# One block of value products for each quad of attention, behind all of its transposes

## Chip, cores and metric

The kernel runs on one core of a Trainium2 chip. The metric is device time in microseconds of one launch, the median of three runs.

## What is computed

One inference step of a small hybrid transformer: 128 context tokens and 512 latent tokens, model width 1024, two layers, each with three groups of attention heads side by side and a squared-ReLU MLP of width 4096. All in float32. The part that matters here is the attention:

```
# differential heads (4): two softmaxes, one subtracted from the other
p1 = softmax(q1 @ k1.T * scale);  p2 = softmax(q2 @ k2.T * scale)
o  = (p1 - lam * p2) @ v
# windowed heads (8, two key/value heads): context keys + three blocks of 128 keys + a sink logit
p  = softmax(concat([s_ctx, s_band, s_sink]));  o = p[ctx] @ cv + p[band] @ vb
# latent heads (4): keys and values unpacked from a compressed vector
o  = softmax(q @ k.T * scale) @ v
```

A latent token reads 128 context keys and 512 latent keys (five blocks of 128), in the windowed heads three or four blocks. Each head's values have 64 columns.

## The kernel before

Everything up to the MLP of a layer is a plan: tasks are given in a serial order with their engine, an assumed duration, a priority and the tiles that they read, write and open. `Plan.run` (line 165) places them on the engines by readiness and priority, and emits each engine's instructions in the order in which the tasks start in that plan. An engine then runs its list strictly in order. A task's own instructions stay together. Rings (`RINGS`, line 46) limit how many tiles of a kind are open at once: `PT` 3, `t` (PSUM buffers for transposes and small products) 3, `o` (PSUM output) 1, `s` (scores) 2, `quad` (probabilities) 2, `E` 4.

The attention is cut into quads (`quad`, line 968): two heads times two blocks of 128 queries. In a layer there are eight quads of windowed, four of differential and four of latent heads. For each of the four (head, query block) pairs of a quad PE makes scores into `s` (lines 1000, 1008, 1016), DVE takes the maximum (1030), ScalarE the exponential with its sum (1038), and the row is scaled (965) or, in differential heads, the second softmax is subtracted (1060). The probabilities lie in `e_`, a tile of the ring `quad`.

Then come the key blocks of the quad, in `slots` (line 1069): five for differential and latent heads, four for windowed ones (three that both query blocks read, and one that only one reads). For each slot there are three tasks: `tr` on PE transposes two or four 128x128 blocks into a `t` buffer (line 1081), DVE or ScalarE evicts them into a `PT` buffer (the copy in line 1092; the profile has it under the helper's lines 376 and 374), and `pv` on PE adds the value products of the slot to O (line 1085): for each head one product, whose 64 output columns fill one half of O's partitions. Each such product is two records in the trace. `tr` and `pv` have the same priority, so the plan takes `pv` of a slot as soon as it is ready. O (ring `o`) is opened by the first `pv` and evicted after the last (line 1097 or the split in line 1100). The context's own queries have their own small path (`context`, line 1139).

Work of low priority fills PE's gaps: conditioning vectors (`conditioning`, lines 551 and 556) and parts of the output projection (`w_out`, lines 517 to 519). All DMA is issued from SyncE's queue (`dma`, line 379). The MLP behind the plan is written out in order and keeps PE busy throughout.

Of the kernel before, what the change touches and what calls it, by code (L numbers as in the profile page):

```python
# [17 lines left out]
PSUM = bass.MemoryType.PSUM  # L18

P = 128  # L20
DEPTH = 2
D = 1024
# [4 lines left out]
EPS = 1e-6  # L27
# [3 lines left out]
# columns of the input projection that go through one PSUM bank together  # L31
# [3 lines left out]
# key blocks of the windowed heads, [cache | L0..L3 | cache]: first column and block numbers per query block  # L35
# [9 lines left out]
# buffers of each ring  # L45
RINGS = {"E": 4, "X": 5, "PT": 3, "B": 8, "h": 4, "mix": 3, "quad": 2, "QK": 4, "wr": 3, "wh": 4, "wl": 4, "zin": 2, "sq4": 2,
         "stt": 10, "osb": 1, "Kc": 1, "ds": 2, "sm": 4, "rsq": 3, "Vsw": 1, "Vda": 1, "Vml": 1, "ckT": 1, "kz": 1,
         "s": 2, "t": 3, "o": 1, "z": 4}
# rings that share the tiles of one, and rings whose tiles are opened in the order of the plan or of priority
SHARE = {"h": "B", "mix": "B", "quad": "B", "QK": "B"}  # L50
IN_ORDER = {"h", "mix", "quad", "QK", "Vml", "Kc", "ds", "osb", "zin", "sq4", "wr", "wh", "wl"}
# microseconds: what one engine's result takes to reach another, the start of a transfer, bytes per microsecond
# [5 lines left out]
# How a layer is run: the engines of the hi and lo parts of operands and of the softmax's scaling, the priorities of  # L58
# transposes and of the preparation of operands, and the order of the parts: N conditionings (cN), half the query
# blocks of two windowed (s), differential (d) or latent (m) heads, their preparation (D, V, M), output projection (w)  # L60
# [35 lines left out]
class Slot:  # L96
    """A tile that one task opens and that is free again behind its last user."""
# [19 lines left out]
class Plan:  # L117
    """Orders the instructions of a phase: tasks are given in a serial order with what they read and write;
    run() places them on the engines by readiness and priority, and emits them in the order they start."""
# [7 lines left out]
    def held(self, ring, t):  # L127
        """A tile that is open already."""
        s = Slot(ring, None, t)
        self.slots.append(s)  # L130
        return s
# [33 lines left out]
    def run(self):  # L165
        """Tiles are opened ahead of the plan's order only where every task before them in that order can still
        have its own, so the order always ends."""
        free = dict(RINGS)
# [10 lines left out]
        rings = {}  # L179
# [22 lines left out]
        def blocked(t):  # L202
            """The ring that has no tile for a task yet."""
            need = {}
            for s in t.alloc:
                for q in s.rings:
                    need[q] = need.get(q, 0) + 1
            if "s" in need and z_left[0]:
                return "z"
            for q, c in need.items():  # L210
                if free[q] < c:
                    return q
            for q, c in need.items():
                before = [s for s in live[q] if not s.open and s.first < t.n]
                if before and (q in IN_ORDER or (q == "t" and t.prio >= 2e6 and free[q] == c)):
                    return q
                if not before:
                    continue
                ahead = [s for s in live[q] if s.open]
                for s in before:  # L220
                    n = sum([x.first <= s.first and x.last >= s.first for x in live[q]])
                    n += sum([x.first > s.first for x in ahead])
                    if n + c > RINGS[q]:
                        return q
            return None
# [9 lines left out]
        # the banks of "z" become those of "s"  # L235
# [14 lines left out]
        # the tensor engine's clock halves behind a window of little work, until a busy one  # L250
# [88 lines left out]
def tile_hybrid_step(ctx: ExitStack, tc: tile.TileContext, i, o):  # L339
# [25 lines left out]
    def add(*a, **k):  # L365
        return cur[0].add(*a, **k)
# [17 lines left out]
    def split(n, hi, lo, src, r, w, prio, scale=None, hi_alloc=(), lo_alloc=(), sb=None, extra=0.0):  # L384
        """hi = f32r(src * scale), lo = src * scale - hi: together the exact float32 value. All arguments are
        functions that give the operands. sb: the engines of hi and lo for a source in SBUF."""
        def f_hi(e):
            if e is S:
                S.activation(out=hi(), in_=src(), func=AF.Copy, scale=1.0 if scale is None else scale)  # L389
            else:  # L390
                e.tensor_copy(hi(), src())

        def f_lo(e):
            if scale is None:
                sub(e, lo(), src(), hi().bitcast(F32))
            else:
                e.scalar_tensor_tensor(out=lo(), in0=src(), scalar=scale, in1=hi().bitcast(F32),
                                       op0=ALU.mult, op1=ALU.subtract)

        wh, wl = w  # L400
        for eng, f, dur, rd, wr, al in (
                (sb[0] if sb else "A", f_hi, {"A": tA(n) + extra, "V": tV2(n)}, list(r), wh, hi_alloc),
                (sb[1] if sb else "V", f_lo, {"V": tV(n), "G": tG(n)}, list(r) + [wh], wl, lo_alloc)):
            if len(eng) > 1:
                add(eng, {e: dur[e] for e in eng}, f, r=rd, w=[wr], alloc=al, prio=prio)
            else:
                e = {"A": S, "V": V, "G": G}[eng]
                add(eng, dur[eng], lambda f=f, e=e: f(e), r=rd, w=[wr], alloc=al, prio=prio)
# [34 lines left out]
    # the sinks as three bfloat16 parts on the first three partitions, that ones sum up again  # L443
# [59 lines left out]
    def load_split(src, n, prio, k=1, load_prio=None, after=(), sb=None):  # L503
        """Weights as hi and lo slots; views with k feature tiles."""
# [10 lines left out]
    def mm3(out, w, a, first, last):  # L515
        """out += whi*ahi + whi*alo + wlo*ahi, w stationary."""
# [8 lines left out]
    def conditioning(l, sec, f0, prio, nf=2, wide=False):  # L525
        """nf feature tiles of one section."""
# [52 lines left out]
    def rsqrt(ms, n, r, prio, scale=1.0, eps=None):  # L579
        """Returns a function that gives y, and what its readers read."""  # L580
# [33 lines left out]
    def stat(st, k, hf, prio):  # L614
        """One feature tile's part of the sums of squares of a half of the tokens: all but the last tile are summed
        before the matrix product over the partitions."""
# [24 lines left out]
    def rstd(st, hf, rb, prio):  # L641
        """1/rms of the half's tokens, the same on all partitions, into PSUM."""
# [27 lines left out]
    def emit_h(l, n, hf, rb, h, k, prio):  # L670
        """h = x * rstd * A + B as hi + lo."""
# [86 lines left out]
    def projection(l, h):  # L758
        """Token-major input projection, with norms, rotary positions and the operands of the heads."""
# [14 lines left out]
        # caches  # L774
# [193 lines left out]
    def quad(l, kind, u, hd, vt, vcols, mix, kt_mix, pr_, hs, at):  # L968
        """Half pr_ of the query blocks of two heads; half 0 also takes the context's own queries."""
# [8 lines left out]
        for y in range(2):  # L978
            for x in range(2):
# [11 lines left out]
                for j in range(2 if kind == "da" else 1):  # L991
# [20 lines left out]
                    else:  # L1012
                        def scores(s=s, h=h, q=q, n=n, a=a, tiles=tiles, w=w, we=we):
# [4 lines left out]
                            # a bank of its own starts anew; the scores' own bank has this column unwritten  # L1018
# [55 lines left out]
        for z, (kt, have) in enumerate(slots):  # L1074
# [8 lines left out]
            def pv(z=z, kt=kt, c=c, w=w, PT=PT):  # L1083
                for x in range(2):
                    T.matmul(out=O.t[64 * x:64 * x + 64, c:c + w], lhsT=vt.t[:, kt, vcols[x]:vcols[x] + 64],  # L1085
                             rhs=PT.t[:, x, c:c + w], start=(z == 0), stop=(z == ns - 1))

# [5 lines left out]
            add("P", 0.23 * len(have), pv, r=[PT, (vt, kt)], w=[] if z == 0 else [O], alloc=[O] if z == 0 else [], prio=p_t)  # L1093
# [10 lines left out]
        if kind == "da":  # L1104
            # per-head rms norm; rows carry their softmax sum s1, so eps becomes eps * s1^2
# [108 lines left out]
    def da_prep(l, w, u, at):  # L1214
# [15 lines left out]
        for t in (1, 2, 3, 4, 0):  # L1230
            for a in range(2):
# [9 lines left out]
                def part(x, st=st, a=a):  # L1241
                    """The queries as [hi lo hi lo], the keys as [hi hi lo lo]."""
# [39 lines left out]
    def mla_prep(l, w, u, u0, kvw, at):  # L1282
# [8 lines left out]
        # rotary part of the keys: the same rows for every head  # L1291
# [135 lines left out]
    def up_out(gt, f, hf, puv, r):  # L1427
        """Squared ReLU of a feature tile, as hi + lo, in four stages."""
# [9 lines left out]
    def first_up(l, h, Gt, ws, after):  # L1438
        """The first half of the tokens goes feature tile by feature tile of h, into four accumulators."""
# [71 lines left out]
    # ================= layers =================  # L1511
    dn, Gt_last = None, None
    for l in range(DEPTH + 1):
        with ExitStack() as es:
# [52 lines left out]
            # attention  # L1567
# [49 lines left out]
            # norm and the first feature tiles  # L1617
# [20 lines left out]
        with ExitStack() as es:  # L1638
# [14 lines left out]
            # the banks of scores and outputs of the attention come first: the others are still read  # L1653
# [169 lines left out]
```

## Time and profile before

| | us |
|---|---|
| median of three runs | 1797.12 |
| lowest and highest run | 1793.64, 1797.24 |
| span of the profiled execution | 1794.8 |
| PE busy in it | 1701.9 |
| DVE busy in it | 1111.0 |
| ScalarE busy in it | 731.7 |

The span goes from the first to the last instruction of the profiled execution. In layer 0 the attention fills roughly 178 to 433 us, in layer 1 1055 to 1296 us; between and behind them lie the MLPs (475 to 890 us and 1345 to 1770 us, PE busy throughout). A busy PE is not PE at its peak: matmuls overlap in the pipeline and their ends are modelled, so the cost of one is read from the distance of starts, or from the pieces of the chain, which don't overlap. "PE" is the matmul, "PEld" its weight load; a table by stretch has PE, PEld, DVE, ScalarE (ACT) and GpSimd (POOL) in this order, then the granted TensorE clock (1.00 is the 2.4 GHz level, 0.50 the 1.2 GHz one), the DMA share and GB/s. The chain is the work that ended last, followed back from the end, at each step to what released it.

### The profile page before, as it was taken

How to read it: one execution, taken by the hardware profiler on the slowest of the kernel's cores; microseconds unless marked ns; L12 is line 12 of the kernel's file. 1: busy time of each engine (PE TensorE's matmuls, PEld its weight loads, DVE VectorE, ACT ScalarE, POOL GpSimd, SP SyncE). 2: the span in 40 equal slices, each digit the busy share in tenths (PEclk: the TensorE clock that was granted, in tenths of full speed). 3: DMA queues.
4: the chain of work that ended last, by engine and by line, in shares of the span. 5: the costliest groups of instructions: out<-in, count | busy, mean ns of one | idle time of the engine just before them, and what ended most of it. 6: DMA issues, size and time to landing. Idle time of an engine off the chain costs nothing.

```text
span 1794.8 us, 29510 instructions
## 1 busy us (share of the span) xinstructions
PE 1701.9 (95%) x11371; PEld 1509.7 (84%) x11371; DVE 1111.0 (62%) x2870; ACT 731.7 (41%) x1624; POOL 322.2 (18%) x284
## 2 busy tenths in 40 slices
PE   6999998999999999999989999989989999999997
PEld 4787567577999999999978766766879999999997
DVE  5875568887654444444594748988784444444446
ACT  4533566774432222322243336766653222321231
POOL 2310037422200000000063201653350000000000
PEclk9999999999999999999999999989999999999999
DMA  8323453431122222222212324303212222222221
GB/s 308 108 68 118 157 162 92 133 126 60 52 71 83 71 71 83 71 75 72 78 52 83 94 96 128 119 26 113 71 60 72 82 71 83 72 71 75 79 71 60
DMA packets 67388, 163.22 MB, mean 91 GB/s; under 512 B 6896, under 2 KB 31280, under 8 KB 67248
## 3 DMA queue, kind: packets, MB, share of 16 engines
q1 hardware_dynamic: 67248, 161.34, 27.7%
q8 instruction: 90, 1.47, 0.3%
q14 instruction: 50, 0.41, 0.1%
HBM read 153.15 MB, written 8.16 MB: 90 GB/s over the span
## 4 chain that ended last, share of the span: by engine, by line
PE 80%; DVE 14%; ACT 2%; issue 2%; POOL 1%; DMA 1%; SPq 0%; DVEq 0%; ACTq 0%; POOLq 0%
PE pu L518 15%; PE pu L519 15%; PE pu L517 15%; PE O L1085 4%; PE pt L1081 3%; PE pz L810 3%; PE pz L812 3%; PE pz L811 3%; PE po L517 2%; PE pa L551 2%; PE po L518 2%; PE po L519 2%; PE sps L1016 2%; PE sps L1008 1%; DVE stt L1030 1%
## 5 line engine op out<-in xcount | busy, mean ns | idle before, releaser
L517 PE MATMUL pu<-hh,wh 128*128 128x256 f32 (+1 forms) x960 | 299.2, 312 | 0.0
L519 PE MATMUL pu<-hh,wl 128*128 128x256 f32 (+1 forms) x960 | 299.1, 312 | 0.0
L518 PE MATMUL pu<-hl,wh 128*128 128x256 f32 (+1 forms) x960 | 299.0, 311 | 0.0
L519 PE MATMUL pu<-Gt,wl 128*128 128x384 f32 (+1 forms) x896 | 277.5, 310 | 0.0
L518 PE MATMUL pu<-Gt,wh 128*128 128x384 f32 (+1 forms) x896 | 277.4, 310 | 0.0
L517 PE MATMUL pu<-Gt,wh 128*128 128x384 f32 (+1 forms) x896 | 277.0, 309 | 0.0
L715 DVE SCALAR_TENSOR_TENSOR xT<-pu,ada,xT 128x128 f32<-128x128 f32 x336 | 126.9, 434 | 175.0 <-PE pu L519 175.0
L374 ACT ACTIVATE wh<-wr 128x1024 fp32r<-128x1024 f32 x116 | 120.5, 1050 | 217.8 <-PE pu L518 179.5
L1434 DVE SCALAR_TENSOR_TENSOR r<-pu,r 128x256 f32<-128x256 f32 (+1 forms) x128 | 57.4, 486 | 231.0 <-ACT r L1433 229.3
L1433 ACT ACTIVATE r<-pu 128x256 f32<-128x256 f32 (+1 forms) x128 | 49.6, 435 | 343.5 <-PE pu L519 339.6
L382 DVE TENSOR_TENSOR wl<-wr,wh 128x1024 fp32r<-128x1024 f32 x132 | 161.2, 1223 | 34.5 <-ACT wh L374 22.7
L519 PEld LDWEIGHTS pu<-hh,wl 128*128 128x128 f32 x960 | 180.6, 188 | 0.0
L518 PEld LDWEIGHTS pu<-hl,wh 128*128 128x128 f32 x960 | 180.5, 188 | 0.0
L517 PEld LDWEIGHTS pu<-hh,wh 128*128 128x128 f32 x960 | 180.4, 188 | 0.0
L628 POOL TENSOR_TENSOR sq<-sq 128x256 f32<-128x256 f32 (+1 forms) x22 | 18.3, 831 | 887.4 <-ACT sq L622 886.6
L518 PEld LDWEIGHTS pu<-Gt,wh 128*128 128x128 f32 x896 | 168.5, 188 | 0.0
L517 PEld LDWEIGHTS pu<-Gt,wh 128*128 128x128 f32 x896 | 168.4, 188 | 0.0
L519 PEld LDWEIGHTS pu<-Gt,wl 128*128 128x128 f32 x896 | 168.4, 188 | 0.0
L382 POOL TENSOR_TENSOR wl<-wr,wh 128x1024 fp32r<-128x1024 f32 (+2 forms) x46 | 107.4, 2338 | 194.6 <-ACT wh L389 179.4
L810 PE MATMUL pz<-wh,hh 128*128 128x512 f32 (+1 forms) x320 | 131.3, 410 | 5.2 <-DVE hh L376 4.1
L1030 DVE TENSOR_REDUCE stt<-sps 128x1 f32<-128x640 f32 (+2 forms) x160 | 117.0, 737 | 23.6 <-PE sps L1023 16.8
L812 PE MATMUL pz<-wh,hl 128*128 128x512 f32 (+1 forms) x320 | 125.7, 393 | 0.1
(288 smaller groups left out, 3433.5 us busy)
## 6 DMA issues: line engine op xcount, KB each, us to landing
wr<-in_w_ada SPq DMA_DIRECT2D x80, 512.0 KB, 4.2
wr<-in_w_up SPq DMA_DIRECT2D x64, 512.0 KB, 3.5
wr<-in_w_down SPq DMA_DIRECT2D x64, 512.0 KB, 3.5
wr<-in_w_in SPq DMA_DIRECT2D x24, 512.0 KB, 3.5
wr<-in_w_out SPq DMA_DIRECT2D x16, 512.0 KB, 4.0
wq<-in_w_ada SPq DMA_DIRECT2D x6, 1024.0 KB, 11.7
wr<-in_w_in SPq DMA_DIRECT2D x8, 416.0 KB, 3.2
xT<-in_xT SPq DMA_DIRECT2D x4, 640.0 KB, 6.6
```

The source lines that it names most:

```text
L374: S.activation(out=out, in_=in_, func=AF.Copy)
L382: eng.tensor_tensor(out=out, in0=a, in1=b, op=ALU.subtract)
L517: T.matmul(out=out, lhsT=w[0], rhs=a[0], start=first, stop=False)
L518: T.matmul(out=out, lhsT=w[0], rhs=a[1], start=False, stop=False)
L519: T.matmul(out=out, lhsT=w[1], rhs=a[0], start=False, stop=last)
L715: V.scalar_tensor_tensor(out=xT[:, m, a:b], in0=po[:, a - a0:b - a0], scalar=ada[l][:, sec, m, s:s + 1], in1=xT[:, m, a:b], op0=ALU.mult, ...
L810: T.matmul(out=out, lhsT=h_at(h, "h", k, tk), rhs=wh[:, x], start=(k == 0), stop=False)
L811: T.matmul(out=out, lhsT=h_at(h, "h", k, tk), rhs=wl[:, x], start=False, stop=False)
L812: T.matmul(out=out, lhsT=h_at(h, "l", k, tk), rhs=wh[:, x], start=False, stop=(k == KD - 1))
L1030: add("V", tV(we) - 0.01, lambda st=st, j=j, view=view: V.tensor_reduce(out=st.t[:, j:j + 1], in_=view(), axis=AX.X if kind == "sw" else A ...
L1085: T.matmul(out=O.t[64 * x:64 * x + 64, c:c + w], lhsT=vt.t[:, kt, vcols[x]:vcols[x] + 64], rhs=PT.t[:, x, c:c + w], start=(z == 0), stop=( ...
L1434: lambda: V.scalar_tensor_tensor(out=r, in0=puv[:, :w], scalar=0.0, in1=r, op0=ALU.max, op1=ALU.mult),
```

## The change

The value products of all slots of a quad become one task behind the transposes and evictions of all slots. The ring `PT` goes from 3 to 8 buffers. The plan's assumed duration of that task is 0.15 + 0.255 us for each (slot, query block), where a slot's task had 0.23 us for each query block before. O is opened by the one task. The scratch space that the program sets aside for dynamic DMA is set to 1024. Comments are dropped; nothing else differs.

```diff
-RINGS = {"E": 4, "X": 5, "PT": 3, "B": 8, ...
+RINGS = {"E": 4, "X": 5, "PT": 8, "B": 8, ...
...
         p_t = PAR["tr"] + at
-        for z, (kt, have) in enumerate(slots):
+        pvs = []
+        for kt, have in slots:
             pt, PT = mk("t", [P, 2, 256], F32, "pt"), mk("PT", [P, 2, 256], F32, "PT")
             c, w = have[0] * P, len(have) * P
...
-            def pv(z=z, kt=kt, c=c, w=w, PT=PT):
-                for x in range(2):
-                    T.matmul(out=O.t[64 * x:64 * x + 64, c:c + w], lhsT=vt.t[:, kt, vcols[x]:vcols[x] + 64],
-                             rhs=PT.t[:, x, c:c + w], start=(z == 0), stop=(z == ns - 1))
...
-            add("P", 0.23 * len(have), pv, r=[PT, (vt, kt)], w=[] if z == 0 else [O], alloc=[O] if z == 0 else [], prio=p_t)
+            pvs.append((kt, c, w, PT))
+
+        def pv():
+            for z, (kt, c, w, PT) in enumerate(pvs):
+                for x in range(2):
+                    T.matmul(out=O.t[64 * x:64 * x + 64, c:c + w], lhsT=vt.t[:, kt, vcols[x]:vcols[x] + 64],
+                             rhs=PT.t[:, x, c:c + w], start=(z == 0), stop=(z == ns - 1))
+
+        add("P", 0.15 + sum(0.255 * len(have) for _, have in slots), pv,
+            r=[q for kt, _, _, PT in pvs for q in (PT, (vt, kt))], alloc=[O], prio=p_t)
...
-    nc = bacc.Bacc("TRN2", target_bir_lowering=False, num_devices=1)
+    nc = bacc.Bacc("TRN2", target_bir_lowering=False, num_devices=1, dynamic_dma_scratch_size=1024)
```

## Rows read from the trace of the kernel before

**Rows 1.** The page, part 1: busy us, share of the span, instructions.

```profile
PE 1701.9 (95%) x11371; PEld 1509.7 (84%) x11371; DVE 1111.0 (62%) x2870; ACT 731.7 (41%) x1624; POOL 322.2 (18%) x284
```

**Rows 2.** Engines by stage: stretch, its us, busy us (instructions), granted clock, DMA.

```profile
178.00:287.00 109.00, 102.10 (x791) 66.99 (x792) 71.87 (x188) 68.22 (x185) 31.63 (x33) 0.97 0.44 142
287.00:378.00 91.00, 83.61 (x634) 59.02 (x634) 79.05 (x207) 65.17 (x164) 46.17 (x50) 1.00 0.43 135
378.00:433.00 55.00, 54.15 (x390) 44.17 (x390) 43.78 (x113) 30.37 (x66) 10.04 (x8) 1.00 0.18 57
1055.00:1140.00 85.00, 82.54 (x663) 51.77 (x662) 69.93 (x187) 56.62 (x158) 15.99 (x17) 1.00 0.45 143
1140.00:1247.00 107.00, 93.80 (x666) 74.12 (x666) 96.00 (x223) 73.18 (x188) 61.46 (x60) 0.95 0.24 76
1247.00:1296.00 49.00, 48.99 (x362) 39.00 (x359) 36.35 (x96) 30.02 (x65) 12.29 (x8) 1.00 0.23 76
```

**Rows 3.** Chain that ended last, by line: whole run, 287:378, 1140:1247 us.

```profile
by line: PE pu L518 15.3%; PE pu L519 15.3%; PE pu L517 15.3%; PE O L1085 3.6%; PE pt L1081 3.4%; PE pz L810 3.0%; PE pz L812 2.8%; PE pz L811 2.8%; PE po L517 2.0%; PE pa L551 1.9%; issue 1.9%; PE po L518 1.8%; PE po L519 1.8%; PE sps L101
by line: PE pt L1081 9.3%; PE O L1085 9.1%; PE sps L1008 5.6%; DVE stt L1030 5.0%; PE pa L551 5.0%; POOL xT L1412 4.5%; issue 3.2%; PE sps L1000 3.2%; ACT quad L1038 2.7%; ACT tm L1408 2.6%; DVE quad L1060 2.4%; DVE ada L562 2.2%; DVE Kml L
by line: DVE stt L1030 9.8%; PE pt L1081 7.8%; PE O L1085 6.1%; issue 4.4%; DVE quad L1060 4.2%; PE sps L1000 4.1%; PE po L517 4.0%; PE po L518 3.8%; PE po L519 3.7%; PE pk L1349 2.8%; DVE rsq L596 2.7%; DVE ds L1050 2.7%; DVE PT L376 2.4%;
```

**Rows 4.** Line 1085 alone in the stretches of group 2: differential stages, sum.

```profile
287.00:378.00 91.00, 12.41 (x82) 4.25 (x82) 1.00 0.43 135
1140.00:1247.00 107.00, 12.18 (x84) 4.72 (x84) 0.95 0.24 76
sum 496.00, PE 80.35 PEld 33.35; mean PE 13.39 PEld 5.56
```

**Rows 5.** Chain in order of time, 1258 to 1272 us: start, us, what.

```profile
1262.23 0.88 PE pt L1081 x8
...
1263.99 1.01 PE O L1085 x8
1265.00 1.02 PE pt L1081 x8
...
1270.05 0.58 PE O L1085 x4
1270.63 0.38 PE po L517
...
1271.37 0.18 PE po L517
```

**Rows 6.** Chain in order of time, 1086 to 1095 us.

```profile
1089.95 1.81 PE pt L1081 x14
1091.76 1.66 PE O L1085 x16
```

**Rows 7.** PE in order of time, line 1085: first and last of 93 runs.

```profile
181.77 1.98 PE L1085 MATMUL O<-PT,Vsw 128*64 128x256 f32 x8
...
1293.91 0.65 PE L1085 MATMUL O<-PT,Vml 128*64 128x256 f32 x4
```

**Rows 8.** Line 1085, idle time before it: released by, us, times.

```profile
  DVE PT L376: 3.0, 7
  ACT PT L374: 1.6, 6
```

**Rows 9.** Groups by line and shape, DVE: busy us, mean ns, idle before.

```profile
L1030 DVE TENSOR_REDUCE stt<-sps 128x1 f32<-128x640 f32 x96 | 77.5, 814 | 6.1 <-PE sps L1000 4.0 <-PE sps L1008 1.8
L376 DVE COPY PT<-pt 128x512 f32<-128x512 f32 x61 | 41.3, 687 | 22.2 <-PE pt L1081 19.5 <-PE O L1085 2.5
```

**Rows 10.** Engines around a fall of the clock; columns as in group 2.

```profile
1181.50:1185.00 3.50, 1.45 (x8) 1.07 (x8) 3.30 (x11) 2.34 (x6) 1.55 (x3) 1.00 0.10 28
1185.00:1188.30 3.30, 2.15 (x8) 1.76 (x9) 3.17 (x6) 1.64 (x6) 3.22 (x3) 0.51 0.00 0
1188.30:1191.70 3.40, 3.40 (x15) 2.97 (x15) 2.09 (x6) 2.55 (x5) 0.33 (x2) 0.50 0.00 0
```

More of the change, by code (lines that the diff above doesn't have):

```diff
@@ L43 @@
 N_CST = 900
-RINGS = {"E": 4, "X": 5, "PT": 3, "B": 8, "h": 4, "mix": 3, "quad": 2, "QK": 4, "wr": 3, "wh": 4, "wl": 4, "zin": 2, "sq4": 2,
+RINGS = {"E": 4, "X": 5, "PT": 8, "B": 8, "h": 4, "mix": 3, "quad": 2, "QK": 4, "wr": 3, "wh": 4, "wl": 4, "zin": 2, "sq4": 2,
          "stt": 10, "osb": 1, "Kc": 1, "ds": 2, "sm": 4, "rsq": 3, "Vsw": 1, "Vda": 1, "Vml": 1, "ckT": 1, "kz": 1,
```

## Prediction

> **What bounds the kernel now.** I read the page's busy shares first: TensorE (PE) is busy 95% of the span and no other engine more than 62% [rows 1]. The change touches only the attention part, so I cut that out by stage: windowed, differential and latent heads of layer 0 (178 to 287, 287 to 378, 378 to 433 us) and of layer 1 (1055 to 1140, 1140 to 1247, 1247 to 1296 us). In the windowed and latent stages PE is busy 94 to 100% and DVE 66 to 82%; in the two differential stages DVE is busy 87% and 90% and PE 92% and 88% [rows 2]. So there are two kinds of stage. In four of them PE sets the pace; in the two differential ones PE and DVE take turns.
>
> The chain of work that ended last says the same. The value products (line 1085, output O) make up 3.6% of the whole chain, 64.6 of 1794.8 us; in the two differential stages they are 9.1% of 91 us and 6.1% of 107 us, 8.3 and 6.5 us [rows 3]. Line 1085 is busy 80.35 us in the six stages together, 12.41 and 12.18 us of it in the differential ones [rows 4]. So (64.6 - 14.8) / (80.35 - 24.59) = 89% of this work lies on the chain in the four PE stages, and 14.8 / 24.59 = 60% in the differential ones.
>
> What the change can save is seen only between instructions. In the chain's pieces a run of value products takes 0.58 us for one key block (4 records) and 1.01 us for two (8 records) [rows 5], and 1.66 us for the three and a half blocks of a whole windowed quad (16 records) [rows 6]. From 0.58 to 1.01 is 0.43 us for a block, from 1.01 to 1.66 it is 0.65 / 1.5 = 0.43 us again. A run thus costs 0.43 us a block plus **0.15 us once**. The piece behind a run pays as well: eight transposes take 1.02 us behind a run and 0.88 us elsewhere, the first matmul of an output projection 0.38 us behind a run and 0.18 us elsewhere [rows 5]. That is 0.14 to 0.20 us, and I take 0.14, as a transpose is the commonest successor. **One entry and exit of value products costs 0.29 us**, whatever its length. What is special about it is visible in the shape: these matmuls fill 64 of the 128 output columns and two of them run beside each other, which the operations around them don't do.
>
> **The change, part by part.** *Fewer runs.* The PE timeline has 93 runs of line 1085, from 181.77 to 1293.91 us [rows 7]: 18 and 18 windowed, 17 and 14 differential, 13 and 13 latent (layer 0 and 1). Afterwards each of the 32 quads has one (8, 4 and 4 in each layer), because a task of the plan is emitted without anything between its instructions. So 20 windowed, 23 differential and 18 latent runs go, 61 in all, worth 61 x 0.29 = 17.7 us of PE time. The number of matmuls and transposes stays.
>
> *What of it lies on the path.* In the four PE stages 38 x 0.29 x 0.89 = 9.8 us. In the differential stages 23 x 0.29 x 0.60 = 4.0 us at most, and nothing if DVE, at 87 to 90%, is late next; I take half, 2.0 us. Together 11.8 us, with 9.8 and 17.7 us as ends (the upper one if all PE time counted).
>
> *The new wait.* A block needs all evictions of its quad, where today each pair of products waits for its own. Queued behind it on PE are the scores of the next quad, and behind those DVE's maxima, ScalarE's exponentials and the next transposes, besides fillers (conditioning, output projection). Today value products stop PE for 3.0 + 1.6 us, 13 times, 0.35 us each [rows 8], out of 144 tasks. From below: if one in eleven of 32 blocks waits as today, 1.0 us is left and 3.6 us are gained. From above: if each of the 32 waits 0.35 us, 11.2 us, 6.6 us more than today. I take two in three, 7.5 us, **3 us more than now**, nearer the upper end, since at the end of a quad no transposes of its own are left to put in front.
>
> *The block's length.* With five key blocks it is 5 x 0.43 + 0.15 = 2.3 us, today at most 1.0 us for such heads. Meanwhile no scores are made. The two score buffers hold work for two maxima of 0.81 us each [rows 9], 1.6 us, so DVE could fall dry by some 0.7 us for a quad. Nothing is added for it: in the PE stages DVE has 18% or more to spare [rows 2], and in the differential ones I count only half of the gain for this reason.
>
> *The ring of eight.* Five evicted blocks of a quad stand until its products have run, which leaves three for the next quad. The score tile of a quad comes free at its last transpose, which no longer waits for products to free a buffer; from zero to a small gain, counted at zero. Three PSUM buffers for transposes stay, so a transpose still waits for evictions. The output bank O opens later; that is free, as nothing else wants it but the context's own product.
>
> *The end of a layer.* The last products end later by the wait for one eviction, 0.69 us [rows 9], and four blocks. Today the last run is at 1293.91 us [rows 7] and PE is busy 48.99 of 49.00 us around it [rows 2], filled with output projection that does not read it. I cost it at nothing; without that cover it is 0.69 + 4 x 0.43 = 2.4 us a layer. The smaller DMA scratch touches no path: every transfer goes through SyncE's queue.
>
> **Sum.** 11.8 - 3.0 = 8.8 us less. The profiled span is 1794.8 us and becomes 1786.0; the median of the runs is 1797.1, 2.3 us above that span, so the time becomes 1788.3 us.
>
> **Rivals.** *All of it counts.* 17.7 us, 1779.4 us. For it: PE is 88% busy or more in every stage, and earlier transposes free the score tile earlier. Against: 60% in the differential stages.
>
> *Absorbed.* The differential stages give nothing and every block waits 0.35 us: 9.8 - 6.6 = 3.2 us, 1793.9 us, hardly to be told from no change (a measurement of this kernel tells about 0.2%, 3.6 us). For it: DVE at 87 to 90%.
>
> *The clock.* In layer 1's differential stage PE is busy only 1.45 of 3.50 us from 1181.5 us, and in the two stretches behind that the granted clock is 0.51 and 0.50, the 1.2 GHz level [rows 10]. Those 6.7 us do the work of half the time, so one such drop costs 3.4 us. Grouped transposes with waits between could bring one more in each layer, 6.8 us: 8.8 - 6.8 = 2.0 us, 1795.1 us. Against it: the longest row of transposes of today, 14 in 1.81 us [rows 6], lies in a stage with a granted clock of 1.00 [rows 2]. The Trainium skill speaks for this rival: "TensorE: Matmul & The Clock Gate", Part 4 (PE-mode transpose), says that transposes don't count as activity for the clock as matmuls do. By that rule a change that puts all transposes together and takes the products out from between them should lower the clock; the row of 14 doesn't show it, so the chance stays small.
>
> *Slower: PE stands at the head of each block.* If the planner finds no other work ready between a quad's last transpose and its block, PE waits for the whole last eviction, 0.69 us [rows 9], 32 times, and with 80% of it on the chain (64.6 / 80.35) that is 17.7 us, against 11.8 saved: 5.9 us slower, 1803.0 us. It decides from 11.8 / (32 x 0.8) = 0.46 us of mean wait. For it: a mean of 0.35 us for those that wait today, and a DVE that in the differential stages may be inside a maximum of 0.81 us when the eviction comes. Against: 131 of 144 product tasks don't wait today.
>
> **How the numbers follow.** Forecast 0.53, all of it 0.13, absorbed 0.12, clock 0.07, slower 0.15. The likeliest gives 1788.3 us. The range goes from 1779 (all of it) past absorbed and clock to 1800, where only the larger part of the slower case is left out. Faster by over 0.2%: 0.53 + 0.13 = 0.66. Within it: 0.12 + 0.07 = 0.19. Slower: 0.15.
>
> **What would show it.** Right: 32 runs of value products (line 1085 today), of about 2.3 us (windowed 1.66 us) in the chain; PE's busy time in the windowed and latent stages shorter by some 10 us with no new idle time; the differential stages shorter by 2 us or so. Wrong: the products' wait for evictions well over 7.5 us in sum (new wait), a clock row of 0.5 that is not there now, differential stages of the same length (absorbed), or a block that takes more than 0.43 us for a key block (then the cost lies not in entering and leaving but in the products themselves). It is also wrong if the plan, which is made anew from changed tasks, moves other work so that PE waits in places that have nothing to do with this; the stages' idle time would show where.

## The result: slower, by 0.6%

The changed kernel takes 1807.75 us (median of 5 runs, 1804.85 to 1811.41), the kernel before, beside it, 1797.24 us. The ratio is 1.0061, with a 95% interval of 1.0045 to 1.0077. The forecast was 1788.3 us, faster; its range ended at 1800. The profiled execution of the changed kernel has a span of 1806.0 us, 11.2 us more than that of before.

The page's part 1 of the changed kernel (busy us, share of the span, instructions) answers to [rows 1]:

```profile
PE 1698.4 (94%) x11371; PEld 1522.9 (84%) x11371; DVE 1111.1 (62%) x2878; ACT 726.1 (40%) x1609; POOL 332.9 (18%) x291
```

PE is busy 3.5 us less, and the span is 11.2 us longer: idle PE time grew by 14.7 us. It also counts against PE that more of its work ran at the 1.2 GHz level. The mean granted clock fell from 0.984 to 0.978.

The value products (now line 1094) look as foretold. The chain in order of time (start, us, what) has these blocks, a windowed one first:

```profile
208.76 1.67 PE O L1094 x16
...
383.50 2.31 PE O L1094 x20
385.81 1.02 PE pt L1082 x8
...
1254.85 2.31 PE O L1094 x20
```

There are 32 of them, 16 with 16 records and 16 with 20. A block of five key blocks takes 5 x 0.43 + 0.15 = 2.3 us, and the transposes behind it still take 1.02 us, as in [rows 5]. So a key block costs what it cost, and the entry is paid once.

The view of line 1094, which answers to [rows 8], shows what PE waited for ahead of it (us, times), and who waited for it:

```profile
  issue: 5.3, 19
who waited for it (us, times):
  ACT mix L389: 13.8, 17
  ACT osb L374: 8.9, 5
```

No eviction (PT) stands in the first list: PE never waits at the head of a block for transposed probabilities. The second list is where something new is: ScalarE waits 8.9 us, five times, to move the output O of a differential quad into `osb`. Before, its row was:

```profile
  ACT osb L374: 0.4, 2
```

Where the time went is seen between landmarks in PE's order of time: the last product of the windowed, the differential and the latent heads, and the first matmul of the MLP's second half ("down"), in us:

| stretch ending at | layer 0 before | after | layer 1 before | after |
|---|---|---|---|---|
| last windowed product (from the last projection) | 100.3 | 94.9 | 86.2 | 81.1 |
| last differential product | 106.6 | 121.3 | 105.7 | 108.8 |
| last latent product | 51.0 | 47.2 | 48.7 | 49.0 |
| first "down" of the MLP | 87.0 | 95.1 | 90.7 | 90.0 |

The windowed stages gave 10.5 us, about what all four PE stages were to give. Not all of it is the grouping: layer 0's stage has the same 748 matmul records as before, but 3.4 us less at half clock, and layer 1's has twelve records of transposes and scores fewer and six of the projection more. In `hold`, below, which keeps every stage's work, these two stages gave 4.1 us and nothing. Then 14.7 + 3.1 us were lost in the differential stages and 8.1 us behind layer 0's last product, where 30 more matmuls of the output projection had been left to do (132 records instead of 102).

Engines by stage after the change, which answers to [rows 2] with the same columns, the bounds moved to the new landmarks:

```profile
178.00:282.00 104.00, 96.00 (x781) 66.83 (x780) 78.67 (x196) 66.64 (x179) 35.04 (x37) 0.98 0.45 144
282.00:388.00 106.00, 90.41 (x637) 67.06 (x638) 81.83 (x203) 64.75 (x161) 53.09 (x55) 0.90 0.41 128
388.00:439.00 51.00, 48.74 (x367) 41.99 (x367) 40.88 (x103) 28.39 (x65) 12.73 (x10) 0.97 0.15 44
1068.00:1148.00 80.00, 78.29 (x657) 52.16 (x657) 64.78 (x182) 54.97 (x151) 16.61 (x17) 1.00 0.47 152
1148.00:1258.00 110.00, 96.77 (x672) 77.02 (x668) 93.62 (x236) 75.07 (x188) 58.32 (x56) 0.94 0.27 81
1258.00:1308.00 50.00, 48.20 (x376) 40.94 (x375) 40.42 (x102) 28.63 (x68) 10.32 (x8) 1.00 0.19 60
```

The second row is the bad one: 15 us longer than its counterpart, DVE busy 77% instead of 87%, and a granted clock of 0.90 instead of 1.00. Two pairs of stretches in it show how the clock falls (columns as above); ahead of the falls at 301.4 and 376.5 us PE was busy 1.35 of 3.40 and 1.77 of 3.50 us:

```profile
350.00:352.60 2.60, 0.83 (x10) 0.33 (x10) 2.50 (x11) 0.82 (x2) 0.43 (x2) 1.00 0.52 181
352.60:356.00 3.40, 3.40 (x24) 1.97 (x18) 1.21 (x5) 2.19 (x6) 1.97 (x2) 0.50 0.62 181
365.00:369.60 4.60, 2.17 (x18) 1.86 (x15) 4.39 (x11) 3.19 (x9) 1.60 (x4) 1.00 0.27 100
369.60:373.00 3.40, 3.40 (x15) 3.01 (x13) 3.40 (x11) 2.71 (x5) 1.37 (x2) 0.51 0.00 0
```

PE is busy 0.83 of 2.60 us and 2.17 of 4.60 us, waiting for DVE and ScalarE, and then works at a granted clock of 0.50 and 0.51. PE's waits in the same stage (us in total, times, longest) show one of the sources; in the kernel before, none of these three is among its ten largest waits there:

```profile
PE sps L1000 <- ACT e L1038: 3.2, 2, 2.6
PE sps L1008 <- ACT e L1038: 2.4, 1, 2.4
PE pt L1082 <- DVE PT L376: 2.3, 2, 2.1
```

Three things are mixed here: the products stand together, they stand later, and every engine's order is another, since the plan was made anew. Where two or three engines may do a task, the plan also chooses the engine, so another plan moves work between DVE, ScalarE and GpSimd, too (their counts above differ from [rows 1]); "order" stands for both below. The experiments take these apart.

### The profile page after: what moved, and what is told of

Read it like the earlier page. It is cut to its first block, busy times and chain, and to the rows that moved or that the text cites. A ratio compares the mean times of both kernels' runs of the same rounds, so it can differ in the third digit from the quotient of the medians.

```text
span 1806.0 us, 29476 instructions
## 1 busy us (share of the span) xinstructions
PE 1698.4 (94%) x11371; PEld 1522.9 (84%) x11371; DVE 1111.1 (62%) x2878; ACT 726.1 (40%) x1609; POOL 332.9 (18%) x291
## 4 chain that ended last, share of the span: by engine, by line
PE 74%; DVE 15%; issue 5%; ACT 2%; DMA 1%; POOL 1%; SPq 0%; DVEq 0%; ACTq 0%; POOLq 0%
PE pu L517 15%; PE pu L518 15%; PE pu L519 15%; PE pt L1082 3%; PE O L1094 3%; PE pz L810 2%; PE pz L812 2%; PE pz L811 2%; PE po L517 2%; PE po L519 2%; PE po L518 2%; PE pa L551 2%; DVE stt L1030 1%; PE sps L1008 1%; DVE xT L715 1%
## 5 line engine op out<-in xcount | busy, mean ns | idle before, releaser
L382 POOL TENSOR_TENSOR wl<-wr,wh 128x1024 fp32r<-128x1024 f32 (+2 forms) x48 | 112.7, 2351 | 188.5 <-ACT wh L389 166.4
```

Source lines behind the costliest of these rows:

```text
L382: eng.tensor_tensor(out=out, in0=a, in1=b, op=ALU.subtract)
```

## Experiments

**The same order, the products together.** In `hold` every engine keeps its work and its order of the kernel before. Only the products of a quad are withheld and issued together at the place of the last slot's; the ring has its eight buffers.

```diff
-                for x in range(2):
...
+                held.append((z, kt, c, w, PT))
+                for z, kt, c, w, PT, x in [q + (x,) for q in held for x in range(2)] if z == ns - 1 else []:
...
```

> The plan of the kernel before, with its order on every engine, except that the value products of a quad are held back and issued together at the place of the last slot's (eight PT buffers in memory, three in the plan). So the runs of value products are 32 and nothing else moves. Theory A (the block is good, the plan made anew is what loses): 1783 to 1789 us, 8 to 14 us under before, since 61 entries and exits at 0.29 us go and about 80% of them lie on the chain. Theory B (a block of 2.3 us behind the last eviction starves DVE and ScalarE of scores, whatever the order around it): 1800 to 1808 us, with the loss in the differential stage of layer 0.

Measured: 1801.29 us against 1798.26, ratio 1.0022 (1.0007 to 1.0036). Its page's part 1:

```profile
PE 1691.9 (94%) x11371; PEld 1516.4 (84%) x11371; DVE 1109.0 (62%) x2870; ACT 730.7 (41%) x1624; POOL 321.4 (18%) x284
```

PE is busy 10.0 us less than before, yet the span (1799.5 us) is 4.7 us longer. So grouping alone, without another order, already turns its gain into a small loss; the rest of the 0.6% goes with the order made anew. The time is in the band of theory B, but the larger loss is not in the stage that the theory names: between the landmarks, layer 0's differential stage is 3.0 us longer than before and layer 1's 6.5 us.

**The parts of the plan.** `ring8` is the kernel before with eight PT buffers in the plan (and the smaller DMA scratch), so the plan may order anew:

```diff
-"X": 5, "PT": 3,
+"X": 5, "PT": 8,
```

> The kernel before with eight PT buffers, in the plan too, and the small DMA scratch; the products stay slot by slot. Theory A: the plan changes in places, so the time moves by some us either way, 1791 to 1803 us. Theory B: no block, so no loss: within 4 us of before, 1793 to 1801 us. A third theory (earlier transposes and evictions by the larger ring crowd out other work) wants 1803 to 1808 us.

Measured: 1806.01 us, ratio 1.0040 (1.0023 to 1.0056). That is in the band of the third theory, by which the larger ring itself costs. But hold_noda, below, has the eight buffers and the small scratch in the order of before and is not slower, so neither costs by being there; what is slower is the plan that eight buffers lead to. `before_c28` changes still less: only the duration that the plan assumes for a pair of products. What is computed stays, and so do the tasks.

```diff
-            add("P", 0.23 * len(have), pv, r=[PT, (vt, kt)],
+            add("P", 0.03 + 0.255 * len(have), pv, r=[PT, (vt, kt)],
```

> The kernel before, products slot by slot, only the plan's assumed duration of a slot's products is 0.03 + 0.255 us for each query block instead of 0.23. The instructions are the same ones; only their order is another. Theory A: a new order alone moves the time by several us, most likely upward: 1800 to 1808 us, with PE waits and falls of the clock in places that before does not have. Theory B: within 4 us of before, 1793 to 1801 us.

Measured: 1814.25 us, ratio 1.0085 (1.0070 to 1.0100). Its page's part 1:

```profile
PE 1708.9 (94%) x11371; PEld 1517.2 (84%) x11371; DVE 1104.6 (61%) x2863; ACT 735.0 (41%) x1621; POOL 334.5 (18%) x297
```

So more than the order differs, other than its expectation says: GpSimd has 13 instructions more than in [rows 1], DVE 7 and ScalarE 3 fewer. This is the strongest single hint on the plan: with slot-by-slot products, the kernel reaches layer 0's last differential product 9.0 us later than the kernel before and the first "down" 14.5 us later; the change does so 9.7 and 14.0 us later. Its differential stage of layer 0 (columns as above) has the same low clock, 0.91, without any grouping:

```profile
269.00:383.00 114.00, 101.32 (x708) 76.90 (x707) 90.81 (x224) 78.30 (x195) 62.78 (x67) 0.91 0.33 105
```

Two versions of the changed kernel with other assumed durations ask the same from the other side, after_c23 in the first added line, after_c366 in the second:

```diff
-        add("P", 0.15 + sum(0.255 * len(have) for _, have in slots), pv,
+        add("P", sum(0.23 * len(have) for _, have in slots), pv,
+        add("P", 0.3 + sum(0.216 * len(have) for _, have in slots), pv,
```

> The change as it is, but the plan assumes 0.23 us for each query block of a quad's products and no 0.15 us once: the same work in a third order. If the order made anew is what loses, and before's order is a lucky one, it lies somewhere in 1798 to 1818 us, with its losses in other stages than the changed kernel's. If the block itself loses in the differential stages, it is at 1803 to 1810 us with the loss in the same place, between the last windowed and the last differential products of layer 0.

> The change with the measured cost of a block in the plan: 0.30 us once and 0.216 us for each query block. Nearly the same sum as in the changed kernel (2.46 against 2.70 us for five key blocks). If small errors of the plan's durations matter little and the structure decides, within 4 us of the changed kernel, 1803 to 1812 us. If each set of durations gives an order with a time of its own, it may lie anywhere in 1795 to 1818 us.

Measured: after_c23 1813.02 us, ratio 1.0092 (1.0071 to 1.0113); after_c366, told what products cost by the traces, 1801.5 us, ratio 1.0018 (1.0004 to 1.0031). In after_c366 layer 0's differential stage takes 95.5 us (121.3 in the change) with no time at half clock, but the stretch behind layer 1's last product takes 102.1 us instead of 90.0, since output projection was left over for it. The durations that the plan assumes thus move the changed kernel by 0.7% and move the loss from one place to another.

**Which quads.** `no_da` is the changed kernel with differential quads slot by slot as before, so that only windowed and latent quads are grouped, with a plan made anew; `no_da_c366` differs from it by the assumed duration alone.

```diff
-            pvs.append((kt, c, w, PT))
+            if kind != "da":
+                pvs.append((kt, c, w, PT))
+                continue
...
+            add("P", 0.23 * len(have), pv1, r=[PT, (vt, kt)], w=[] if z == 0 else [O], alloc=[O] if z == 0 else [], prio=p_t)
```

`hold_noda` groups the same quads, in the order of the kernel before (the edit is shown against hold):

```diff
-                held.append((z, kt, c, w, PT))
-                for z, kt, c, w, PT, x in [q + (x,) for q in held for x in range(2)] if z == ns - 1 else []:
+                held[:] = (held if kind != "da" else []) + [(z, kt, c, w, PT)]
+                for z, kt, c, w, PT, x in [q + (x,) for q in held for x in range(2)] if z == ns - 1 or not (kind != "da") else []:
```

> The change for windowed and latent quads alone; the differential quads keep a product task for each slot. Theory B: the gain of the windowed stages (10 us) and of the latent ones (3 us) stays and the loss of the differential ones goes: 1781 to 1787 us. Theory A: the plan is made anew here too, so the differential stage of layer 0 may be long even without a block in it: 1790 to 1806 us.

> One block for a windowed or latent quad, differential quads slot by slot, plan made anew, as in no_da (1813.7 us), but the plan is told 0.30 us + 0.216 us a block for the products instead of 0.15 + 0.255. Nothing that runs on the chip is another instruction, only the order can differ. Theory 'the order decides' (the same work in the order of the kernel before took 1794.3 us): the time moves by more than 4 us, to anywhere between 1790 and 1809. Rival 'the structure decides': within 4 us of 1813.7, 1810 to 1817.

> Order of before on every engine, products held back to the last slot's place in windowed and latent quads alone. If a held block costs time only where DVE and ScalarE are as loaded as PE (differential stages), what hold gained elsewhere stays and what it lost there goes: 1790 to 1794 us, 3 to 7 us under before. If late products cost as much as the fewer entries save everywhere, 1797 to 1801 us.

Measured: no_da 1813.74 us, above both of its bands, 1.0084 (1.0066 to 1.0102); no_da_c366 1817.56 us, 1.0111 (1.0084 to 1.0137); hold_noda 1794.29 us, 0.9987 (0.9976 to 0.9998). The step from no_da to no_da_c366, 3.8 us, is within the 4 us that were set for "the structure decides", so that pair does not show that the order matters. But hold_noda groups the same quads and is faster than no_da by 0.97%, some 17 us, and only the order lies between them. hold_noda is the one version with all of the work in it that is faster than the kernel before, by 0.13%, at the edge of what these runs can tell.

`hold_da` is its counterpart: only differential quads are grouped, in the order of before (the added lines, which stand in the place of hold_noda's).

```diff
+                held[:] = (held if kind == "da" else []) + [(z, kt, c, w, PT)]
+                for z, kt, c, w, PT, x in [q + (x,) for q in held for x in range(2)] if z == ns - 1 or not (kind == "da") else []:
```

> Order of before, products held back in differential quads alone. By the first theory of the run before (loss in the differential stages): 1802 to 1808 us, 3 us lost in layer 0 and 6 us in layer 1 between the last windowed and the last differential products. By the second: within 3 us of before, 1795 to 1801 us.

Measured: 1806.28 us, ratio 1.0059 (1.0042 to 1.0076). So the loss by grouping lies in the differential quads. In the profiled execution it is seen in layer 1, whose stage is 5.3 us longer than before; layer 0's is 106.7 us against 106.6, not 3 us longer as expected, and stages that hold_da leaves alone differ by up to 1.7 us. What a late block does is seen in a quad of layer 1. First PE's products and ScalarE in order of time in the kernel before (start, us, instruction, idle time before it and what ended it):

```profile
1169.58 1.08 PE L1085 MATMUL O<-PT,Vda 128*64 128x256 f32 x8
...
1172.48 0.65 PE L1085 MATMUL O<-PT,Vda 128*64 128x256 f32 x4
...
1172.59 0.38 ACT L374 ACTIVATE Vml<-pv 128x256 f32<-128x256 f32 x1 [0.64 <-PE pv L1274]
1173.18 0.39 ACT L374 ACTIVATE osb<-O 128x256 f32<-128x256 f32 x1 [0.21 <-PE O L1085]
```

Then the same place in hold_da:

```profile
1170.62 2.38 PE L1086 MATMUL O<-PT,Vda 128*64 128x256 f32 x20
...
1170.72 0.38 ACT L374 ACTIVATE Vml<-pv 128x256 f32<-128x256 f32 x1 [0.51 <-PE pv L1274]
1173.04 0.39 ACT L374 ACTIVATE osb<-O 128x256 f32<-128x256 f32 x1 [1.94 <-PE O L1086]
```

Before, two slots' products ran 3 us ahead of the end, between other work, and only the last slot's 0.65 us were left when its eviction had come. Now all 2.38 us come behind the last eviction. Without the early products the work ahead of the block is done sooner: ScalarE, which works in order, reaches its move of O 1.9 us earlier, stands for 1.94 us, and moves O about when it did before; behind it stand an exponential of the next quad and the next evictions. The loss shows in what follows: the next quad's O is moved 28.59 us after this one, instead of 26.89 us. The other three quads of layer 1 show waits of 1.74, 1.95 and 1.80 us (the profile puts the last one down to a copy on GpSimd), against 0.23 us or less before. That is about the 4 x 0.43 = 1.7 us by which four more slots are late. Layer 0's quads show 0.43, 0.87, 0.02 and 1.99 us, against 0.90 us at most before. In ScalarE's waits of hold_da over the whole run the row is (us, times, longest):

```profile
ACT osb L374 <- PE O L1086: 8.9, 6, 2.0
```

**All but the last slot.** If lateness is the cost, it goes when the last slot stays alone. `but1` issues the products of all slots but the last at the last-but-one slot's place, in the order of before; `mixed` does so in differential quads and holds the others as hold_noda does. but1 against hold:

```diff
-                held.append((z, kt, c, w, PT))
-                for z, kt, c, w, PT, x in [q + (x,) for q in held for x in range(2)] if z == ns - 1 else []:
+                held[:] = (held if not (True) or z < ns - 1 else []) + [(z, kt, c, w, PT)]
+                for z, kt, c, w, PT, x in [q + (x,) for q in held for x in range(2)] if z == ns - 1 or (z == ns - 2 and (True)) else []:
```

> Order of the kernel before on every engine; in each quad the value products of all slots but the last run together at the last-but-one slot's place, the last slot's products stand alone at their own place: 64 runs of products instead of 93 (32 when all are held). Theory 'late products' (what was saved by grouping is lost because all of a quad's products come behind its last eviction, so that ScalarE's eviction of O and the DVE work behind the block stand for 1.7 to 1.95 us more in a differential quad): here only one slot's products are behind the last eviction, as in the kernel before, so 29 x 0.29 us x 0.8 = 6.7 us are kept: 1790 to 1794 us, and the wait of ScalarE for O is within 0.3 us of that before. Rival 'length of a block' (PE makes no scores for 4 blocks x 0.43 us, so DVE starves wherever the block stands): 1797 to 1802 us, and DVE waits behind the block as much as when all are held.

> Order of the kernel before; windowed and latent quads hold all of their products to the last slot's place, differential quads hold all but the last slot's to the last-but-one slot's place. Theory 'late products': the gain of holding in windowed and latent quads alone (3.3 us) plus some of the 23 differential runs: 1788 to 1793 us. Rival 'length of a block' or 'any grouping in the differential stages costs': 1795 to 1802 us.

Measured: but1 1797.62 us, ratio 1.0002 (0.9990 to 1.0015); mixed 1799.77 us, 1.0011 (0.9999 to 1.0023). The trace of but1 has 51 runs of products rather than 64, as blocks often stand right before the last slot's pair. ScalarE's wait for O is gone:

```profile
ACT osb L374 <- PE O L1086: 0.4, 2, 0.2
```

So half of the theory holds. With the wait that longer distance goes, too: from the first to the second move of O in layer 1 it is 26.88 us in but1 and in mixed. But both times lie in the bands of the rivals, not in those of "late products", and in but1 the next distance stays long without a late O: 24.99 us, as in hold_da (24.71), where before has 22.05 and mixed 23.25.

but1 is faster than hold_da by 0.57%, some 10 us, but the two differ in more than the last slot. hold and mixed differ in that slot of the differential quads alone: 0.11%, some 2 us, and their intervals overlap. mixed against hold_noda isolates what is left: the differential quads are grouped without a late O, and it costs 0.24%, some 4 us. So of the 0.35%, 6 us, by which hold is slower than hold_noda, the late O seems to be the smaller part. DVE's waits in layer 1's differential stage (us, times, longest), first hold_noda, then mixed:

```profile
DVE Kda L376 <- PE pt L1250: 1.1, 1, 1.1
DVE PT L376 <- PE pt L1081: 0.8, 2, 0.5
DVE osb L1130 <- PE orb L1118: 0.7, 1, 0.7
...
DVE stt L1030 <- PE sps L1000: 0.6, 3, 0.2
```

```profile
DVE Vml L376 <- PE pv L1274: 1.9, 2, 1.3
DVE stt L1030 <- PE sps L1000: 1.7, 4, 1.1
DVE osb L1130 <- PE orb L1118: 1.3, 1, 1.3
```

While a block runs, PE makes no scores and none of DVE's other operands, and DVE, the busiest engine of this stage beside PE, runs dry. All its waits for PE in that stage sum to 5.5 us in the kernel before, 4.6 in hold_noda, 7.2 in but1, 7.8 in mixed, 9.2 in hold and hold_da and 10.4 in the change. That fits the rival "length of a block", which no run isolates: layer 0's stage shows no such step (9.4 us before, 9.6 in hold_noda, 10.1 in mixed, 8.0 in hold_da), and before_c28, which groups nothing, has 12.5 us in layer 1. What share of mixed's 4 us comes from it and what from the clock (median half-clock time 61.1 us, hold_noda 53.8; by the slope found below, about 2 us) is not settled.

**Is PE time worth anything here?** `twice` adds PE time where the change takes it: the first key block's products of each quad run twice. `skip` takes it away without moving anything: the second key block's products are left out (the last added line below; the others are of twice).

```diff
-                for x in range(2):
+                for n, x in [(0, 0), (0, 1), (1, 0), (1, 1)] if z == 0 else [(1, 0), (1, 1)]:
...
+                             rhs=PT.t[:, x, c:c + w], start=(z == 0), stop=(n == 0 or z == ns - 1))
...
+                for x in range(2) if z != 1 else []:
```

> The kernel before with PE work added where the change takes it away: in each of the 32 quads the first key block's two value products run twice, the first time for nothing (both start the accumulation anew, so the output stays). Order, tasks and number of runs of products stay; 32 x 0.43 = 13.8 us of PE time come in. It measures alone the step 'what of it lies on the path'. If that step was right (89% in the PE stages, 60% in the differential ones): 24 x 0.43 x 0.89 + 8 x 0.43 x 0.60 = 11.3 us slower, some 1809 us, and the gain of grouping was lost to a new cost. If only the part that the grouped windowed and latent quads gave back holds (3.3 us of some 11 us of PE time, 30%): 4 us slower, some 1802 us, and most of the saved PE time was never worth anything. Between 1804 and 1807 both have a share.

> The mirror of twice: the kernel before without the value products of each quad's second key block (this part of the computation is left out); everything else, the order too, stays, and no product moves to a later place. 32 x 0.43 = 13.8 us of PE time go, and 0.29 us with each run of products that had this block alone (about half of 32: 4 to 5 us): 18 us in all, about what the change takes from PE. Theory 'the place' (saved PE time counts as added time did, 96%, as long as no product moves; grouping lost its gain because the products it saves on are moved behind the last eviction, away from the places where PE then waits): 14 to 18 us faster, 1780 to 1784 us. Rival 'the next wait' (PE is kept busy by other work that is only just late, so that less work is not less time wherever it is taken): 3 to 7 us faster, 1790 to 1794 us, and PE's idle time grows by 10 us or more.

Measured: twice 1810.02 us against 1796.85, ratio 1.0072 (1.0058 to 1.0085); skip 1786.94 us against 1797.52, ratio 0.9938 (0.9921 to 0.9955). Part 1 of their pages, twice first:

```profile
PE 1715.1 (95%) x11499; PEld 1519.1 (84%) x11499; DVE 1111.2 (61%) x2870; ACT 731.8 (40%) x1624; POOL 322.2 (18%) x284
```

```profile
PE 1686.0 (94%) x11243; PEld 1498.5 (84%) x11243; DVE 1111.9 (62%) x2870; ACT 731.5 (41%) x1624; POOL 322.1 (18%) x284
```

twice has 13.2 us more PE time than [rows 1] and takes 0.72% = 12.9 us longer: 98% counts. skip has 15.9 us less (87 runs of products instead of 93, not the 16 fewer that its expectation reckoned with) and takes 0.62% = 11.1 us less (8.1 to 14.2): 70% counts (51 to 89%). That lies between the two bands that were set, nearer to "the place". PE time saved in place is worth about 0.7 of itself. By that, hold's 10.0 us were worth 7 us; it lost 4 us instead, so gathering the products in a later place cost some 11 us, if the share holds there.

**The clock.** Time at half clock follows from a run's span and mean granted clock, 2 x (1 - clock) x span. Over 175 runs of all these kernels, each taken against its own kernel's mean, the time grows by 0.30 us for each us at half clock (correlation 0.84). Medians: before 57, hold_noda 54, hold 61, skip 55, but the kernels with a plan made anew 67 to 76, the change 75.9. So the change's 18 us more at half clock go with 18 x 0.30 = 5.5 us, about half of its loss. This is a correlation between runs, not an experiment on the clock, and it may be in part the same time as what the order costs.

## Why the prediction was wrong

*Fewer runs: right in number, the size at the upper end of what came.* There are 32 runs of the foretold length. But 61 x 0.29 = 17.7 us of PE time did not come: in the same order PE's busy time fell by 10.0 us in hold, 0.16 us a run. The other versions in that order range from 0.15 (mixed, 53 runs fewer) over 0.22 (hold_da, 23) to 0.29 us (but1, 42, and hold_noda, 38). These are single executions that differ by up to 21 us at half clock, where the same work takes longer (24 transposes took 4.34 us at 1250.5 us of the change, most of it at half clock; eight take 0.88 us at full clock), so how much of the 0.14 us for "what follows" is real stays open; the entry of 0.15 us is there.

*What lies on the path: borne out.* The forecast took 11.8 of 17.7 us, 67%; skip showed 70%, twice 98%. PE does set the pace, in the differential stages perhaps more than I took: twice made them 1.1 and 1.4 us longer for the 4 x 0.43 = 1.7 us that each got.

*The new wait: on the wrong engine, and the first step that failed.* I priced PE waiting for evictions, 3 us more; PE's wait for PT ahead of products fell from 4.6 us [rows 8] to none. This refutes the slower rival as it was priced, too: the time came near its 1803.0 us, but not by its mechanism. What I left out is who waits for the block: ScalarE stood 8.9 us for O in the change, 0.4 us before. A step that makes PE's work later needed the same question that I asked of PE: what is queued behind the waiting instruction on ScalarE (the next exponentials and evictions) and on DVE?

*The end of a layer, 0.69 + 4 x 0.43 us, "at nothing": the late blocks are the end of every quad, not of a layer.* In windowed and latent quads little was lost by it: of hold_noda's 10.9 us less of busy PE, 0.7 x 10.9 = 7.6 us were due, and 2.3 us (0.13%) came, so some 5 us went in 24 quads, 0.2 us each. In differential quads, where ScalarE moves O for a norm that follows, grouping cost 0.35% (hold against hold_noda) to 0.59% (hold_da), 6 to 10 us in eight quads. ScalarE's waits of 1.74 to 1.95 us in the four of layer 1 are one part of that; without the late slot some 2 us came back, which is not clear of the noise.

*The block's length, "nothing is added": wrong in the differential stages.* I reckoned that DVE could fall dry by 0.7 us a quad, and then let half of a gain stand for it. mixed against hold_noda: some 4 us for eight quads, 0.5 us each, with every O in time; part of it is perhaps the clock, and that DVE's dry time is the rest is argued, not shown.

*The plan made anew: named as a risk, not priced, and the larger step that failed.* It should have been a rival with a chance of its own. hold against the change is 1.0022 against 1.0061: some 7 us of the loss of 11 us go with another order. All seven kernels with an order made anew (ring8, before_c28, no_da, no_da_c366, after_c23, after_c366, the change) were slower than before, by 0.18% to 1.11%, one of them with the products slot by slot and only an assumed duration changed. The plan's other settings stayed those of before; whether a plan set anew for the block would do better was not tried. Which of the moved tasks makes the waits of layer 0's differential stage was not isolated. The ring of eight, counted at zero, was never tried without another change: ring8 alters the order too, and the hold versions group products.

*The clock: the rival's mechanism at work, for another reason.* I expected it from grouped transposes. In hold the transposes stand together, with the products taken out from between them, and its median half-clock time is 61 us against 57. The Trainium skill, "TensorE: Matmul & The Clock Gate", Part 4, says that transposes don't count as activity for the clock as matmuls do. The figures of hold give that rule little weight here: the falls in the change follow stretches in which PE waited, and before_c28, which groups nothing, has them as well.

## What to carry to other kernels

Work of the bottleneck engine that stands between other engines' results is also its filler: before it is gathered into one block, ask for each engine which in-order instruction will wait for the block's end, and what stands behind that. Price the same edit in the old order and in a new one separately: where a planner orders the work, hold the order fixed in one experiment, and change only a constant of the planner in another, to see how much its plan alone moves. And test the share of saved time that counts by adding and by leaving out work in place; here 0.98 and 0.70, while hold's 10 us of PE time, saved by moving work, came with 4 us more in all.

## What the hardware showed beside this

The time grew by 0.30 us for each us at half clock, where 0.5 us is the estimate for a kernel that PE bounds all the time and that gets half of its work done at half clock. And DVE operations on six columns, which took 0.14 to 0.17 us in most places, took up to 1.52 us while GpSimd worked on score tiles. DVE and GpSimd in order of time, in the change:

```profile
297.04 0.15 DVE L597 SCALAR_TENSOR_TENSOR rsq<-rsq 128x6 f32<-128x6 f32 x1
...
297.31 1.24 DVE L598 SCALAR_TENSOR_TENSOR rsq<-rsq 128x6 f32<-128x6 f32 x1
...
298.68 1.52 DVE L596 TENSOR_TENSOR rsq<-rsq 128x6 f32<-128x6 f32 x1
```

```profile
297.19 1.34 POOL L1057 TENSOR_TENSOR e<-e,stt 128x640 f32<-128x640 f32 x1 [0.96 <-DVE rsq L597]
...
298.61 1.57 POOL L1058 TENSOR_TENSOR quad<-quad,e 128x640 f32<-128x640 f32 x1
```

The long ones end with GpSimd's. It is nothing that the change brought: the kernel before has it as well, beside a GpSimd operation of 1.57 us on `quad` that starts at 1233.74 us:

```profile
1233.94 1.39 DVE L596 TENSOR_TENSOR rsq<-rsq 128x6 f32<-128x6 f32 x1
```

In the change it stands just ahead of the clock's fall at 301.4 us; whether it is its cause, or how much it costs, was not tried.
